# ScalarE and accumulating transfers take over the plain sums of the folded w_down chunks

## The chip, the cores and the metric

The kernel runs on one core of one Trainium2 chip. The metric is the device time of one execution in microseconds (us); lower is better. Of the kernel before there are three timed runs: 1345.83, 1346.43 and 1347.23 us, with a median of 1346.43 us. The profile is of one further execution that took 1346.6 us.

## The reference, cut to what matters

One layer on 256 tokens of width 2048, in float32. A mixing sub-layer with three branches makes a new `x`; then comes a squared-ReLU MLP with hidden width 8192, and a final RMSNorm:

```
h2 = rmsnorm(x, g_mlp)
x = x + jnp.square(jax.nn.relu(h2 @ w_up)) @ w_down
return rmsnorm(x, g_final)
```

The change touches only how parts of the product with `w_down` are added to `x`. The per-token factor of the RMSNorm (its square, since the ReLU is squared) is not applied to `h2` but to the sums of the product with `w_down`; it stands in `stat[:, t, 0:1]`, one value a token, for the token halves `t` = 0 and 1 of 128 tokens each.

## The kernel before, in words

All float32 weights are streamed from HBM once, in pieces of 1 MB (class `W`). A piece is loaded by SyncE (L103) into one of three `raw` buffers. It is then split into a high part, cast by ScalarE to float32r (`hi`, L120), and a rest, subtracted by VectorE (`lo`, L121), in two buffers each. TensorE forms three products (high by high, high by rest, rest by high) and sums them in PSUM.

The MLP is cut into four quarters `q` of the hidden width. A quarter has an up stage (16 pieces of `w_up`, tiles `u`, with `settle` at L190 and L192, then the squared ReLU into `av`, then `yact`) and a down stage (16 pieces of `w_down`). The down stage of the quarters 0 to 2 consists of two chunks `c` of 1024 output columns, each run by `down_folded`; quarter 3 has one such chunk, and its other 1024 columns go through `gemm_tok`.

A folded chunk has eight pieces, `p` = 0 to 7. The even ones are ordinary: 24 matmuls of 512 columns into the tiles `dx` (in the code `xs[0]` and `xs[1]`, one a token half, two PSUM banks each). The odd ones use a 2x2 scheme with seven products instead of eight: 21 matmuls, of which nine go into `dx` and twelve into the four banks of `mb` and `ma`. For these pieces VectorE first makes sums of the raw weights (`t`, L110 to L112), and ScalarE and VectorE split those and the raw ones (`th`, `tl`, `hi`, `lo`, L116 and L117). `t`, `th` and `tl` have one buffer each.

PSUM has four tiles of two banks, and one chunk uses all four. At a chunk's end `down_done` (L734) adds each of the four `dx` banks, times the token's factor, to the residual `xres` on VectorE. ScalarE copies the four banks of `mb` and `ma` out: in quarter 0 straight into `macc` (L684), later into a part sum of 128x512 (L687), which an accumulating transfer from GpSimd's queue adds to `macc` (L688). The part sums lie in the two-buffer groups `cr` and `zs` of the pool `tmp`, which `settle` uses too. `sq` and `mg` are two more groups of that pool; `mg` holds `av` in the up stage. After the last quarter's sums `unfold` combines `macc` into `xres`.

Every engine works its instructions in order. That order is laid down when the kernel is built, by a planner that goes by the program's order and by its own estimates of when things are ready; so the order on VectorE and ScalarE isn't exactly that of the code. `next_w` keeps two pieces prepared ahead, and a load is issued only when a `raw` buffer has been read for the last time.

Of the kernel before, what the change touches and what calls it, by code (L numbers as in the profile page):

```python
# [7 lines left out]
F32 = mybir.dt.float32  # L8
F32R = mybir.dt.float32r
AF = mybir.ActivationFunctionType  # L10
ALU = mybir.AluOpType

P = 128
# [10 lines left out]
NQ = 4  # L24
# [22 lines left out]
def hybrid_trunk(ctx: ExitStack, tc: tile.TileContext, xw_d, gmix_d, xtok_d, wst, wtok, wbr, par_d, wpool_d, bgate_d, gfin_d, out_d):  # L47
    nc = tc.nc
# [6 lines left out]
    tmp = ctx.enter_context(tc.tile_pool(name="tmp", bufs=2))  # L55
# [24 lines left out]
    def four(t):  # L80
        return t.rearrange("p a b -> p (a b)").rearrange("p (k n) -> p k n", n=512)
# [60 lines left out]
    def ps_pair(name):  # L142
        return psum.tile([P, 2, 2 * S], F32, name=name, tag="ps")
# [12 lines left out]
    def next_w():  # L156
        while stream and len(ahead) < 2:
            ahead.append(W(*stream.pop(0)))
        return ahead.pop(0)
# [77 lines left out]
    for n, (k0, k1) in enumerate(zip(cuts, cuts[1:])):  # L237
        if 3 <= n < 6:
            t = wraw.tile([P, KT, P], F32, name=f"xw{n}", tag="raw").rearrange("p a b -> p (a b)")
            t = t[:, 0:2 * STEP].rearrange("p (k n) -> p k n", n=STEP)  # L240
        else:
            t = xcut.tile([P, 2, STEP], F32, name=f"xw{n}", tag="xw")
# [22 lines left out]
    for t, k0, k1 in zip(pieces, cuts, cuts[1:]):  # L265
# [10 lines left out]
        for k in ks:  # L276
            for i in range(NF):
                ps, cols = pfirst[i // 2][:, i % 2, :], slice(i * P, i * P + P)
                if not (last and k == KT - 1):
                    nc.tensor.matmul(ps, fhi[:, k, cols], hact[:, k, :], start=k == 0, stop=False)  # L280
        for k in ks:
            for i in range(NF):
                ps, cols = pfirst[i // 2][:, i % 2, :], slice(i * P, i * P + P)
                nc.tensor.matmul(ps[:, S:2 * S], flo[:, k, cols], hact[:, k, 0:S], start=False, stop=False)
        if last:
            for i in range(NF):
                ps, cols = pfirst[i // 2][:, i % 2, :], slice(i * P, i * P + P)
# [151 lines left out]
    for i in range(8):  # L439
        t = tmp.tile([P, 512], F32, name=f"xt{i}", tag=("sq", "cr", "mg", "zs")[i // 2])  # L440
# [170 lines left out]
    for n, width in enumerate((1024, 512, 512)):  # L611
        banks = fresh_banks(width, f"o{at}")
        gemm_tok(merged, banks, width, ALLK, hooks=hooks[n])
        if n == 0:
            xres, part, stat = (res[name] for name in ("xres", "part", "stat"))
        for c in range(width // 512):
            cols = slice(at, at + 512)
# [23 lines left out]
    def mm3(ps, left, right, start=False, stop=False):  # L641
        nc.tensor.matmul(ps, left[0], right[0], start=start, stop=False)  # L642
        nc.tensor.matmul(ps, left[0], right[1], start=False, stop=False)  # L643
        nc.tensor.matmul(ps, left[1], right[0], start=False, stop=stop)  # L644

    def down_folded(q, c):
        xs = [ps_pair(f"dx{q}_{c}_{t}") for t in range(2)]
        mb, ma = ps_pair(f"mb{q}_{c}"), ps_pair(f"ma{q}_{c}")

        def act(k, t):  # L650
            return yact[:, k, t * P:(t + 1) * P], yact[:, k, S + t * P:S + (t + 1) * P]

        for p in range(8):
            w = next_w()
            hi, lo = four(w.hi), four(w.lo)
            if p in FOLD:
                i = FOLD.index(p)
                a11, a12, a22 = act(2 * p, 0), act(2 * p + 1, 0), act(2 * p + 1, 1)
                s1, s2, s3, s4 = ((sact[:, i, 0, n, :], sact[:, i, 1, n, :]) for n in range(4))
                b11, b21, b22 = ((hi[:, n, :], lo[:, n, :]) for n in range(3))  # L660
                t1, t3, t2, t4 = ((w.thi[:, n, :], w.tlo[:, n, :]) for n in range(4))
                first, last = i == 0, i == len(FOLD) - 1
                own = [(xs[1][:, 0, :], a22, t4), (xs[0][:, 0, :], a12, b21), (xs[0][:, 1, :], s4, b22)]
                shared = [(mb[:, 1, :], s1, t1), (mb[:, 0, :], s3, t3), (ma[:, 1, :], s2, t2), (ma[:, 0, :], a11, b11)]
                if last:
                    for ps, left, right in own:
                        mm3(ps, left, right, False, True)
                for ps, left, right in shared:
                    mm3(ps, left, right, first, last)
                if not last:  # L670
                    for ps, left, right in own:
                        mm3(ps, left, right)
            else:
                for k in range(2):
                    for t in range(2):
                        for h in range(2):
                            mm3(xs[t][:, h, :], act(2 * p + k, t), (hi[:, 2 * k + h, :], lo[:, 2 * k + h, :]),
                                p == 0 and k == 0, p == FOLD[-1] - 1 and k == 1 and t == h == 1)
        down_done(xs, 1024, 1024 * c, (1, 0), False)
        for n, m in enumerate((mb, ma)):  # L680
            for h in range(2):
                d = macc[:, c, 2 * (1 - n) + h, :]
                if q == 0:
                    nc.scalar.copy(d, m[:, h, :])  # L684
                    continue
                part_sum = tmp.tile([P, 512], F32, name=f"ps{q}_{c}_{n}_{h}", tag="zs" if n else "cr")
                nc.scalar.copy(part_sum, m[:, h, :])  # L687
                nc.gpsimd.dma_start(d, part_sum, accum_op=ALU.add)  # L688
# [37 lines left out]
    def scaled(t, cols):  # L726
        square_sum(t, cols, cols.start // 512)
        nc.vector.tensor_mul(fin(t, cols), xres[:, t, cols], gfin[:, cols])

    def down_done(banks, width, at, tokens, last):  # L730
        for c in range(width // 512):
            cols = slice(at + 512 * c, at + 512 * c + 512)
            for t in tokens:
                nc.vector.scalar_tensor_tensor(xres[:, t, cols], banks[t][:, c, :], stat[:, t, 0:1],  # L734
                                               xres[:, t, cols], ALU.mult, ALU.add)
                if last:
                    scaled(t, cols)
# [21 lines left out]
    for q in range(NQ):  # L759
# [17 lines left out]
        for c in range(2 if q < NQ - 1 else 1):  # L777
            down_folded(q, c)
# [107 lines left out]
```

## Time and profile before

| | |
|---|---|
| median of three runs | 1346.43 us |
| profiled execution, its own time | 1346.6 us |
| its span, first to last instruction | 1344.1 us |
| TensorE matmuls, busy | 1334.3 us (99%) |
| VectorE, busy | 1010.1 us (75%) |
| ScalarE, busy | 657.6 us (49%) |
| GpSimd, busy | 21.7 us (2%) |
| granted TensorE clock, mean | 0.999 |

Busy time is that of an engine's own instructions; the issue of a DMA by SyncE or ScalarE isn't counted. A wait is an engine's idle time ahead of an instruction, put down to what ended it. The four quarters' stages lie one behind the other from about 644 us on: in quarter 1, for one, the up stage from 818 to 906 us, chunk 0 from 906 to 948 us and chunk 1 from 948 to 990 us.

### The profile page before, as it was taken

To read this page: it belongs to the slowest core of one execution; us is meant where nothing else is said; L and a number is where in the kernel's file an instruction comes from. 1 tells how busy PE (TensorE), PEld (TensorE's weight loads), DVE (VectorE), ACT (ScalarE), POOL (GpSimd) and SP (SyncE) were. 2 spreads that over 40 slices of the span, in tenths; PEclk is the share of its full clock that TensorE was granted. 3 is DMA by queue.
4 is the path that set the end of the run, shared out by engine and by line. 5 is a ranking of instruction groups with operands and counts; after the bars stand their busy time and mean duration, and the time that the engine had idled before them with its cause. 6 is when DMAs were issued, how large, how long until landed. Compare 5 with 4: busy or idle time off the path is not lost.

```text
span 1344.1 us, 16513 instructions
## 1 busy us (share of the span) xinstructions
PE 1334.3 (99%) x6610; PEld 1128.9 (84%) x6610; DVE 1010.1 (75%) x1273; ACT 657.6 (49%) x800; POOL 21.7 (2%) x47
## 2 busy tenths in 40 slices
PE   9999999999999999999999999999999999999997
PEld 8888888888888888888888888888788888888886
DVE  6779888979766465655667996679866799777967
ACT  7544443434454344344545554455554456544554
POOL 0000000000000000000000000000110001100010
PEclk9999999999999999999999999999999999999999
DMA  9655555656556565565555655555775557755582
GB/s 364 229 188 188 188 188 188 206 192 216 192 185 207 212 205 186 188 235 187 173 188 189 211 195 201 182 199 197 224 225 185 196 209 223 246 189 188 192 273 99
DMA packets 43133, 273.11 MB, mean 203 GB/s; under 512 B 4912, under 2 KB 6064, under 8 KB 12464
## 3 DMA queue, kind: packets, MB, share of 16 engines
q1 hardware_dynamic: 39312, 263.93, 56.5%
q0 software_dynamic: 2880, 5.24, 2.2%
q10 hardware_dynamic: 864, 2.89, 0.6%
q8 instruction: 51, 0.84, 0.2%
q14 instruction: 26, 0.21, 0.0%
HBM read 264.71 MB, written 2.10 MB: 198 GB/s over the span
## 4 chain that ended last, share of the span: by engine, by line
PE 93%; DVE 3%; DMA 2%; issue 1%; ACT 0%; POOLq 0%; POOL 0%; DVEq 0%
PE u L124 17%; PE u L127 9%; PE g L511 6%; PE g L512 6%; PE g L510 6%; PE dx L643 4%; PE dx L642 4%; PE dx L644 4%; PE zc L124 3%; PE o L511 2%; PE o L510 2%; PE o L512 2%; DMA raw<-wtok 2%; PE za L124 2%; PE y L511 2%; PE y L512 2%
## 5 line engine op out<-in xcount | busy, mean ns | idle before, releaser
L120 ACT CAST hi<-raw 128x1024 fp32r<-128x1024 f32 x420 | 423.6, 1050 | 435.9 <-PE g L512 134.4
L121 DVE TENSOR_TENSOR lo<-raw,hi 128x1024 fp32r<-128x1024 f32 x420 | 501.7, 1220 | 176.8 <-ACT hi L120 176.7
L124 PE MATMUL u<-hact,hi 128*128 128x512 f32 x1024 | 245.4, 391 | 0.0
L124 PEld LDWEIGHTS u<-hact,hi 128*128 128x128 f32 x1024 | 187.8, 188 | 36.9 <-ACT ps L687 0.4
L510 PE MATMUL g<-hi,hact 128*128 128x512 f32 x384 | 149.9, 390 | 0.0
L512 PE MATMUL g<-hi,hact 128*128 128x512 f32 x384 | 149.4, 389 | 0.0
L511 PE MATMUL g<-lo,hact 128*128 128x512 f32 x384 | 149.4, 389 | 0.0
L127 PEld LDWEIGHTS u<-hact,lo 128*128 128x128 f32 x1024 | 131.4, 191 | 5.1
L127 PE MATMUL u<-hact,lo 128*128 128x256 f32 x1024 | 133.0, 283 | 0.0
L643 PE MATMUL dx<-lo,yact 128*128 128x512 f32 x252 | 98.8, 392 | 0.2 <-DVE lo L121 0.2
L642 PE MATMUL dx<-hi,yact 128*128 128x512 f32 x252 | 98.9, 392 | 0.0
L644 PE MATMUL dx<-hi,yact 128*128 128x512 f32 x252 | 98.4, 391 | 0.0
L329 DVE SCALAR_TENSOR_TENSOR va<-upad,par,va 128x256 f32<-128x256 f32 x180 | 86.8, 482 | 3.4
L510 PEld LDWEIGHTS g<-hi,hact 128*128 128x128 f32 x384 | 72.1, 188 | 15.0
L511 PEld LDWEIGHTS g<-lo,hact 128*128 128x128 f32 x384 | 72.1, 188 | 14.9
L512 PEld LDWEIGHTS g<-hi,hact 128*128 128x128 f32 x384 | 72.1, 188 | 14.8
L116 ACT CAST th<-t 128x1024 fp32r<-128x1024 f32 x56 | 57.5, 1052 | 33.9 <-issue 16.5
L117 DVE TENSOR_TENSOR tl<-t,th 128x1024 fp32r<-128x1024 f32 x56 | 67.1, 1221 | 8.2 <-ACT th L116 8.2
L192 DVE TENSOR_TENSOR zs_u<-u,cr_u 128x512 f32<-128x512 f32 x32 | 22.1, 691 | 60.6 <-ACT cr_u L190 60.6
L190 ACT COPY cr_u<-u 128x512 f32<-128x512 f32 x32 | 18.8, 588 | 90.6 <-PE u L124 83.4
L642 PEld LDWEIGHTS dx<-hi,yact 128*128 128x128 f32 x252 | 47.3, 188 | 11.5 <-ACT ps L687 0.4
L643 PEld LDWEIGHTS dx<-lo,yact 128*128 128x128 f32 x252 | 47.3, 188 | 10.5 <-DVE lo L121 0.6
(219 smaller groups left out, 1898.1 us busy)
## 6 DMA issues: line engine op xcount, KB each, us to landing
raw<-wtok SPq DMA_DIRECT2D x128, 1024.0 KB, 4.8
raw<-wst SPq DMA_DIRECT2D x93, 1024.0 KB, 4.9
raw<-wbr SPq DMA_DIRECT2D x16, 1024.0 KB, 4.9
xw<-xw SPq DMA_DIRECT2D x7, 768.0 KB, 8.1
macc<-ps POOLq DMA_DIRECT2D x20, 256.0 KB, 7.7
bias<-bgate SPq DMA_DIRECT2D x6, 512.0 KB, 3.6
xt<-xtok SPq DMA_DIRECT2D x8, 256.0 KB, 9.5
xres<-xtok ACTq DMA_DIRECT2D x1, 2048.0 KB, 9.4
```

The source lines that it names most:

```text
L117: fg[0] = nc.vector.tensor_sub(l, r, h.bitcast(F32))
L120: fg[1] = nc.scalar.copy(self.hi[:, ks], self.raw[:, ks])
L121: fg[0] = nc.vector.tensor_sub(self.lo[:, ks], self.raw[:, ks], self.hi[:, ks].bitcast(F32))
L124: nc.tensor.matmul(ps, w.hi[:, k, :], act[:, ak, :], start=start, stop=stop)
L127: nc.tensor.matmul(ps[:, S:2 * S], w.lo[:, k, :], act[:, ak, 0:S], start=False, stop=False)
L329: nc.vector.scalar_tensor_tensor(va[:, i, :], upad[:, i, k:k + S], pcol(C_WDW + i * KA + k), va[:, i, :], ALU.mult, ALU.add)
L510: nc.tensor.matmul(banks[t][:, c, :], left, hi[:, i, cols], start=first, stop=False)
L511: nc.tensor.matmul(banks[t][:, c, :], left, lo[:, i, cols], start=False, stop=False)
L512: nc.tensor.matmul(banks[t][:, c, :], rest, hi[:, i, cols], start=False, stop=last)
L642: nc.tensor.matmul(ps, left[0], right[0], start=start, stop=False)
L643: nc.tensor.matmul(ps, left[0], right[1], start=False, stop=False)
L644: nc.tensor.matmul(ps, left[1], right[0], start=False, stop=stop)
```

## The change

In `down_folded`, for the quarters 0 to 2, the call of `down_done` is replaced. For each of the four `dx` banks ScalarE now writes the bank times the token's factor into a 128x512 buffer `own`, and a transfer from GpSimd's queue adds that buffer to the 512 columns of `xres`. The buffers come from the groups `sq` (token half 1) and `mg` (token half 0), two each. Quarter 3 is as it was.

```diff
--- before.py
+++ after.py
@@ -676,7 +676,15 @@
                         for h in range(2):
                             mm3(xs[t][:, h, :], act(2 * p + k, t), (hi[:, 2 * k + h, :], lo[:, 2 * k + h, :]),
                                 p == 0 and k == 0, p == FOLD[-1] - 1 and k == 1 and t == h == 1)
-        down_done(xs, 1024, 1024 * c, (1, 0), False)
+        if q < NQ - 1:
+            for h in range(2):
+                for t in (1, 0):
+                    own = tmp.tile([P, 512], F32, name=f"ox{q}_{c}_{t}_{h}", tag="sq" if t else "mg")
+                    nc.scalar.activation(own, xs[t][:, h, :], AF.Copy, scale=stat[:, t, 0:1])
+                    cols = slice(1024 * c + 512 * h, 1024 * c + 512 * h + 512)
+                    nc.gpsimd.dma_start(xres[:, t, cols], own, accum_op=ALU.add)
+        else:
+            down_done(xs, 1024, 1024 * c, (1, 0), False)
         for n, m in enumerate((mb, ma)):
             for h in range(2):
                 d = macc[:, c, 2 * (1 - n) + h, :]
```

## Rows read from the trace of the kernel before

**Rows 1.** The page: busy us (share of span) and instructions of an engine.
```profile
PE 1334.3 (99%) x6610; PEld 1128.9 (84%) x6610; DVE 1010.1 (75%) x1273; ACT 657.6 (49%) x800; POOL 21.7 (2%) x47
```
**Rows 2.** Tile dx, all chunks: idle before its instructions (us, times), by releaser.
```profile
  DVE lo L121: 0.9, 2
  ACT ps L687: 0.4, 2
  DVE xres L734: 0.3, 1
  ACT macc L684: 0.2, 1
```
**Rows 3.** Lines L734, L753, L688: duration in ns min/median/max; L688's landing.
```profile
L734 DVE SCALAR_TENSOR_TENSOR xres<-dx,stat,xres x28: 740/744/752, 771.8 to 1292.6; 128x512 f32<-128x512 f32 x28
...
L753 ACT ACTIVATE xres<-xres,stat x2: 722/726/729, 1333.4 to 1338.5; 128x512 f32<-128x512 f32 x2
...
L688 POOL DMA_DIRECT2D macc<-ps x20: 869/1220/1647, 947.6 to 1294.3; - x20
...
DMA to landing us min/median/max: 5.7/7.7/14.8
```
**Rows 4.** ScalarE's order of time, quarter 1, chunk 0 to 1 (start, us, [idle before]).
```profile
942.97 2.00 ACT L120 CAST hi<-raw 128x1024 fp32r<-128x1024 f32 x2 [3.45 <-PE dx L644]
946.45 1.07 ACT L687 COPY ps<-mb 128x512 f32<-128x512 f32 x2 [1.48 <-PE mb L644]
...
950.26 1.51 ACT L116 CAST hi<-raw 128x1536 fp32r<-128x1536 f32 x1
```
**Rows 5.** DMA queues in 952:962: packets, MB, share of 16 engines.
```profile
q0 software_dynamic: 571, 1.04, 57.6%
q1 hardware_dynamic: 261, 1.88, 48.2%
```
**Rows 6.** The chain of waits in 896:975: start, us, what.
```profile
944.72 0.74 DVE xres L734
945.47 2.28 DVE lo L121 x2
947.76 6.28 DMA raw<-wtok
...
957.66 7.56 DMA raw<-wtok
965.32 1.24 DVE t L110
...
967.91 1.23 DVE lo L121
```
**Rows 7.** Issues in 784:785.5, then 1129:1130, then 953:958 (KB each, median us to landing).
```profile
raw<-wtok SPq DMA_DIRECT2D x1, 1024.0 KB, 5.0
...
raw<-wtok SPq DMA_DIRECT2D x1, 1024.0 KB, 6.3
...
raw<-wtok SPq DMA_DIRECT2D x2, 1024.0 KB, 7.9
```
**Rows 8.** The same places of quarters 0 and 2: ScalarE and VectorE in order of time.
```profile
774.40 1.07 ACT L684 COPY macc<-mb 128x512 f32<-128x512 f32 x2 [1.48 <-PE mb L644]
1119.11 1.07 ACT L687 COPY ps<-mb 128x512 f32<-128x512 f32 x2 [1.48 <-PE mb L644]
...
793.28 2.35 DVE L121 TENSOR_TENSOR lo<-raw,hi 128x1024 fp32r<-128x1024 f32 x2
1138.68 2.35 DVE L121 TENSOR_TENSOR lo<-raw,hi 128x1024 fp32r<-128x1024 f32 x2
```
**Rows 9.** The next up stage, quarter 2: GpSimd's issues, their landing, VectorE in order of time.
```profile
989.47 3.59 POOL L688 DMA_DIRECT2D macc<-ps  x4 [38.09 <-ACT ps L687]
...
DMA to landing us min/median/max: 5.7/6.7/8.6
...
1001.80 0.69 DVE L192 TENSOR_TENSOR zs_u<-u,cr_u 128x512 f32<-128x512 f32 x1 [2.78 <-ACT cr_u L190]
```

## The prediction

> **What bounds the kernel now.** I read the page's first part first. TensorE's matmuls are busy 1334.3 us, 99% of the span, beside 75% for VectorE and 49% for ScalarE [rows 1]. So what the change does to the other engines counts only where TensorE then waits, or stops waiting. The second view is the idle time ahead of the instructions on `dx`, the tile whose eviction is changed. Over all seven folded chunks TensorE or its weight loads stood idle for 0.9 + 0.4 + 0.3 + 0.2 = 1.8 us there [rows 2]. Of this 0.3 us is for VectorE's adds to `xres` (L734), which the change removes; 0.6 us is for ScalarE's copies, because a new chunk's `dx` may lie in the banks that these set free; 0.9 us is for `lo`, the prepared weights. Nothing like the VectorE time removed can come back: 1.8 us is the most that better evictions could give here.
>
> The third view is the chain of waits through quarter 1. It does not lead along TensorE there but runs in a loop of weight load, VectorE's sums `t`, VectorE's `lo` and the next load: each load is issued when `lo` has read the buffer that the load will fill (945.47 + 2.28 gives 947.75, and the next load starts at 947.76) [rows 6]. At 967.91 the `lo` of an ordinary piece starts late, because VectorE took the sums of the next folded piece first (965.32) and these had waited for a load of 7.56 us. That is where TensorE's 0.9 us for `lo` arose. So this loop has no slack to spare in chunk 1 of quarter 1, and a slower load there becomes TensorE time.
>
> **The change part by part.**
>
> *VectorE.* It loses 3 quarters x 2 chunks x 4 = 24 adds of 0.744 us [rows 3], 17.9 us of 1010. On the path stands just the first one of a chunk's end: 0.74 us at 944.72, ahead of the `lo` that releases a load [rows 6]. The other three of the four stood behind that `lo`. So the gain on the loop is 0 to 0.74 us at each change from chunk 0 to 1; I take 0.7, as the chain has it.
>
> *ScalarE.* It gains 24 activations of 128x512 out of PSUM with a factor per token. That shape with such a factor isn't in the trace from PSUM. The plain copy out of PSUM takes 1.07 us for two, 0.53 each [rows 4], and the activation with a factor out of SBUF takes 0.726 [rows 3]. I take 0.65, between them; four are 2.1 to 2.9 us, say 2.6. ScalarE is idle for 1.48 us between the casts that end at 944.97 and the first `mb` copy [rows 4], and the last ordinary sums are done by then, as the plain order of the code has them ahead of `mb` and `ma`. That hides 1.5 us; 0.6 to 1.4 us are left, say 1.1. Behind them wait the `mb` and `ma` copies, then `th` and `hi` of the next folded piece, the last of which ends at 951.77 [rows 4] and would end at about 952.9. With it the `lo` after it moves, which releases the load that follows. Net of VectorE's 0.7 the loop shifts by -0.1 to +0.7 us, say +0.4, at each of the three changes from chunk 0 to 1.
>
> *PSUM banks.* The `dx` banks now come free by ScalarE's order, not VectorE's. TensorE's waits for banks were 0.9 us in all [rows 2]; I leave them as they are, with 0 to 0.5 us a chunk for the range in place of their present 0.1 to 0.3.
>
> *GpSimd.* It gains 24 issues of about 1.22 us [rows 3]. Nothing waits for that engine here but its own transfers.
>
> *The transfers.* This is the part with a price. In 952:962 the four accumulating transfers of one chunk end took 57.6% of 16 engines for 10 us, that is 5.8 us of all of them, and with the weight loads' 48.2% the engines were full: the sum is over 100% [rows 5]. The loads beside them took 7.56 us, and 2 x 7.9 - 7.56 = 8.2 us, where one without such company took 5.0 [rows 7]. The change adds as much again at six chunk ends: 24 transfers, 6 x 5.8 = 35 us of all engines. Where does this reach TensorE?
>
> Quarter 1, chunk 1: the loop shifts by 0.4, and the decisive load, 7.56 us now, may take 7.56 to 8.2, as its neighbour did [rows 7]; there is no slack. That is -0.1 to +1.4 us; I take 1.0, nearer the upper end since the company lasts longer.
>
> Quarter 2, chunk 1: the same `lo` starts at 1138.68. The first copy of `mb` tells how far the chunks lie apart: 1119.11 - 946.45 = 172.66 us. So this `lo` was 967.91 + 172.66 - 1138.68 = 1.9 us earlier in its chunk than in quarter 1, where TensorE waited at most 0.9; the slack is about 1.0 us [rows 2, 6, 8]. The load took 6.3 us [rows 7]. A longer stay of 0 to 1.9 (to 8.2) and the shift of 0.4 make 0.4 to 2.3, less 1.0: 0 to 1.3. I take 0.8.
>
> Quarter 0, chunk 1, which has no accumulating transfers now: 946.45 - 774.40 = 172.05 apart, so the `lo` at 793.28 is 2.6 us early, slack 1.7 [rows 6, 8]. Its load would go from 5.0 to between 6.3 and 7.9 [rows 7]: +1.3 to +2.9, with the shift 1.7 to 3.3, less 1.7: 0 to 1.6. I take 0.5.
>
> *The up stage behind chunk 1.* The `macc` transfers now queue behind four others on GpSimd's queue. Their part sums lie in the groups `cr` and `zs`. At the start of quarter 2 the four were issued from 989.47 to 993 and landed 5.7 to 8.6 us after their issue, so by 1000 or so; `zs_u` is written at 1001.80 [rows 9]. With up to 5.8 us in front of them they land by 1006, so this instruction may wait up to 4 us, and behind it on VectorE wait `av` and the `lo` of coming pieces. VectorE was idle for 2.78 us ahead of it [rows 9], so the delay falls in a loose stretch: 0 to 1.5 us of TensorE in quarters 1 and 2 each, and 0 in quarter 0, whose `macc` is copied. I take 0.05 each, nearest to the rows, which show no wait there now.
>
> *Where the trace and a page differ.* The 256 KB transfers of the kernel before took 5.7 to 14.8 us, median 7.7, from issue to landing [rows 3]. The Trainium skill, in "DMA: Bandwidth & Descriptors", section "Anatomy of one DMA — SWDGE (gpsimd) path", fits such a transfer with 2.0 us plus its bytes over 436,000, which an estimate makes 2.6 us for 256 KB, or 2.4 us of data for four. By that page the added transfers would hold the engines 2.4 us an end instead of 5.8, and the sum below would be about +1 instead of +2.4. The measured shares decide.
>
> *The sum.* 1.0 + 0.8 + 0.5 + 0.1 = +2.4 us. The profiled execution took 1346.6 us, so 1349.0; the median of the runs is 0.17 less, so **1348.8 us**. A change of less than 0.2% (2.7 us) can't be told from none on this kernel, so the forecast is: no change that can be told, with a lean to slower. The bounds of the terms above add up to -0.1 on the low side, with all waits for banks (0.9) gone -1.0, and on the high side, with 6 x 0.25 more for banks, to 1.4 + 1.3 + 1.6 + 3.0 + 1.5 = 8.8.
>
> **The rivals.**
>
> *The transfers push the loads back in full.* If the transfer engines work off what GpSimd has queued before they go on with a load, the decisive load moves by the whole 5.8 us of the added four. Then quarter 1 loses 5.8 + 0.4 = 6.2, quarter 2 loses 6.2 - 1.0 = 5.2, quarter 0 loses 6.2 - 1.7 = 4.5: +15.9, 1362 us, slower. It decides from the point where the delay exceeds the slack, 1 to 2 us. For it: in 953:958 a load was 3.2 us late, most of the span of the four transfers [rows 5, 7]. Against it: with 5.8 us of such work the loads lost 2.6 and 3.2 us, not 5.8, and TensorE's waits for `lo` stayed under 1 us. The Trainium skill, in the same page, section "Queues, rings and completion order", has each transfer engine take turns between its queues, a packet at a time, which speaks against it, and no run here shows the turns by themselves. Half of this effect would give +8, about 1354.
>
> *The lighter VectorE loosens the loop.* 17.9 us less on VectorE, and loads issued 0.7 us earlier, could make good what the transfers take, and the waits of [rows 2] go: 0 to -1.8 us, about 1345.5. For it: one of the removed adds is on the chain. Against it: `th` and `hi` of the same stretch are ScalarE's, which gets the work.
>
> *The up stage waits for its buffers.* 1.5 us in two quarters on top of the forecast: +5.4, 1351.8, slower. For it: landing by 1006 against 1001.80. Against it: four PSUM tiles let TensorE run on while `zs_u` is late.
>
> **How the numbers follow.** The forecast, +0.3 to +2.7: 0.42. The loads pushed back, in part or in full: 0.32. The up stage: 0.14. The lighter VectorE: 0.12, of which 0.04 for more than 2.7 us, which the waits in the trace don't hold but an order that the planner changes elsewhere might. So faster 0.04, same 0.42 + 0.08 = 0.50, slower 0.46. The forecast's own range is 1346.7 to 1349.1. The range for 8 in 10 goes from 1345.4 (the sum of the low bounds) to 1356, which takes in the sum of all upper bounds (1355.2) and the push-back up to some 60%; left out are the full push-back and a gain beyond 1.0 us.
>
> **What the profile after would show.** Right: no L734 in quarters 0 to 2, 24 ScalarE activations of 0.59 to 0.73 us, twice the software queue's share behind each chunk, loads of 7 to 9 us there, and TensorE waits for `lo` of 1 to 3 us in sum. Wrong, on the slow side: loads over 10 us and TensorE idle by several us at the third to fifth piece of chunk 1, or VectorE waiting for a DMA at `zs_u`. Wrong, on the fast side: the waits on `dx` gone and a span at or under 1344 us. What would make it wrong altogether is an order on VectorE or ScalarE that the planner changes far from the chunk ends.

## The result and the profile after

The changed kernel takes 1361.64 us (median of four runs, 1360.31 to 1362.80) against 1346.13 us for the kernel before on the same chip. It is slower by 15.5 us, well above the range that was given. The medians' ratio is 1.0115; the recorded estimate is 1.0119, with a 95% interval of 1.0107 to 1.0131. The profiled execution took 1361.13 us, with a span of 1359.4.

The page of the kernel after, busy us of the engines, the queue of GpSimd's transfers (q0; that of the loads is q1), and the median time to landing:

```profile
PE 1339.0 (99%) x6610; PEld 1132.1 (83%) x6610; DVE 993.9 (73%) x1249; ACT 671.2 (49%) x824; POOL 43.2 (3%) x71
...
q0 software_dynamic: 6336, 11.54, 4.7%
...
xres<-ox POOLq DMA_DIRECT2D x24, 256.0 KB, 8.6
...
macc<-ps POOLq DMA_DIRECT2D x20, 256.0 KB, 14.7
```

The change does what it says: VectorE lost 16.2 us, ScalarE gained 13.6, and the software queue moves 11.54 MB. TensorE is still busy for 99% of the span, but the `macc` transfers land 14.7 us after their issue instead of 7.7 [rows 3].

TensorE's 6610 matmuls stand in the same order in both traces, so the start of each can be set against its start before. The distance moves at four places only (worked out from the start times in the two timelines):

```
stretch                           after minus before, us    lost
up to quarter 1, chunk 0          -1.2 (-0.8 of it from the first loads on)
quarter 1, chunk 1, fifth piece   -1.2 ->  2.1              3.3
up stage of quarter 2, 4th piece   2.1 ->  6.2              4.1
quarter 2, chunk 1, fifth piece    6.2 -> 10.8              4.6
up stage of quarter 3, 4th piece  10.7 -> 15.2              4.5
```

That is 16.5 us in four losses of 3.3 to 4.6 us. Quarter 0 loses nothing. What TensorE waited for, in the kernel after (us in total, times, longest):

```profile
PE u L127 <- DVE lo L121: 5.0, 4, 2.3
PE dx L643 <- DVE lo L121: 4.6, 2, 2.7
```

**In chunk 1** it is the loop of [rows 6]. VectorE's order of time there:

```profile
960.66 1.22 DVE L117 TENSOR_TENSOR tl<-t,th 128x1024 fp32r<-128x1024 f32 x1
966.58 1.23 DVE L110 TENSOR_TENSOR t<-raw 128x1024 f32<-128x1024 f32 x1 [4.70 <-DMA raw<-wtok]
967.84 0.69 DVE L111 TENSOR_TENSOR t<-t,raw 128x512 f32<-128x512 f32 x1
968.45 2.35 DVE L121 TENSOR_TENSOR lo<-raw,hi 128x1024 fp32r<-128x1024 f32 x2
```

VectorE waits 4.70 us for the load of the folded piece, and the `lo` that TensorE needs next stands behind that wait. The loads themselves, issued at 956.76 and 1136.61, and the queues' shares in 952:962 (as in [rows 5]):

```profile
raw<-wtok SPq DMA_DIRECT2D x1, 1024.0 KB, 9.7
...
raw<-wtok SPq DMA_DIRECT2D x1, 1024.0 KB, 10.5
...
q0 software_dynamic: 769, 1.41, 79.0%
q1 hardware_dynamic: 165, 1.24, 30.6%
```

The decisive load takes 9.7 us where it took 7.56, and in quarter 2 10.5 where it took 6.3 [rows 7]. GpSimd's transfers hold 79% of the engines' time in a stretch where they held 57.6%. Within it the shares change. In 953:957 a load was issued at 953.4, and the loads had next to nothing (a share is a sum of packet times and can exceed 100%):

```profile
q0 software_dynamic: 447, 0.81, 112.2%
q1 hardware_dynamic: 1, 0.01, 0.5%
```

The kernel before has such a stretch too: in its 954:957 the transfers have 110.7%, and no packet of a load begins, though one was issued at 953.7. The larger difference lies behind it. In 958:966 the loads have 67.8% and the transfers 37.1%, where it was 87.9% and 12.0% before.

**In the up stage** it is the buffers of `settle`. VectorE, ScalarE and TensorE at the start of quarter 2, in order of time:

```profile
998.75 2.36 DVE L121 TENSOR_TENSOR lo<-raw,hi 128x1024 fp32r<-128x1024 f32 x2 [1.93 <-ACT hi L120]
1011.25 0.69 DVE L192 TENSOR_TENSOR zs_u<-u,cr_u 128x512 f32<-128x512 f32 x1 [10.14 <-DMA macc<-ps]
1014.32 3.49 DVE L121 TENSOR_TENSOR lo<-raw,hi 128x1024 fp32r<-128x1024 f32 x3
...
1005.65 0.59 ACT L190 COPY cr_u<-u 128x512 f32<-128x512 f32 x1 [5.99 <-DMA macc<-ps]
...
1013.86 1.29 PE L127 MATMUL u<-hact,lo 128*128 128x256 f32 x8 [1.91 <-DVE lo L121]
```

ScalarE's first copy waits 5.99 us and VectorE's first sum 10.14 us until a part sum's transfer has landed and its buffer is free. The `lo` of coming weights queue behind that sum, and TensorE runs dry. The four transfers here (L696, issued from 992.7 to 997.8), from issue to landing:

```profile
DMA to landing us min/median/max: 12.8/15.1/17.2
```

**After each stall the clock falls.** Windows of the kernel after: length, busy us (instructions) of PE, PEld, DVE, ACT and POOL, TensorE's granted clock, share of the transfer engines, GB/s:

```profile
967.00:969.50 2.50, 0.79 (x4) 0.30 (x2) 2.46 (x3) 1.04 (x1) 0.00 (x0) 1.00 0.53 206
969.50:974.00 4.50, 4.28 (x12) 3.38 (x13) 4.35 (x6) 2.42 (x2) 0.00 (x0) 0.62 0.48 153
...
1013.50:1018.50 5.00, 4.20 (x19) 3.74 (x20) 4.31 (x5) 1.72 (x2) 0.00 (x0) 0.66 0.38 118
...
1150.00:1155.00 5.00, 4.68 (x14) 3.69 (x14) 4.85 (x6) 2.42 (x2) 0.00 (x0) 0.66 0.51 170
...
1194.60:1199.50 4.90, 4.27 (x20) 3.78 (x21) 4.19 (x5) 1.64 (x3) 0.00 (x0) 0.65 0.41 122
```

A mean of 0.62 to 0.66 means that TensorE ran part of the stretch at 1.2 instead of 2.4 GHz. TensorE's order of time shows it: the matmuls of 512 columns are 0.23 us apart before the stall, then 0.42 to 0.43, and 0.23 again:

```profile
967.16 0.39 PE L644 MATMUL dx<-hi,sact 128*128 128x512 f32 x1
967.39 0.40 PE L642 MATMUL dx<-hi,yact 128*128 128x512 f32 x1
969.72 0.50 PE L643 MATMUL dx<-lo,yact 128*128 128x512 f32 x1 [1.94 <-DVE lo L121]
...
971.82 0.63 PE L643 MATMUL dx<-lo,yact 128*128 128x512 f32 x1
972.25 0.63 PE L644 MATMUL dx<-hi,yact 128*128 128x512 f32 x1
...
974.17 0.39 PE L643 MATMUL dx<-lo,yact 128*128 128x512 f32 x1
974.39 0.39 PE L644 MATMUL dx<-hi,yact 128*128 128x512 f32 x1
```

The price is (1 - 0.62) x 4.5 = 1.7 us of work at full clock, and (1 - 0.66) x 5 = 1.7 at the other places: 6.8 us of the 16.5. The stalls themselves cost the other 9.7.

### The profile page after: what moved, and what is told of

It reads as the page before. It is cut to its first block, busy times and chain, and to the rows that moved or that the text cites. A ratio compares the mean times of both kernels' runs of the same rounds, so it can differ in the third digit from the quotient of the medians.

```text
span 1359.4 us, 16583 instructions
## 1 busy us (share of the span) xinstructions
PE 1339.0 (99%) x6610; PEld 1132.1 (83%) x6610; DVE 993.9 (73%) x1249; ACT 671.2 (49%) x824; POOL 43.2 (3%) x71
## 3 DMA queue, kind: packets, MB, share of 16 engines
q0 software_dynamic: 6336, 11.54, 4.7%
## 4 chain that ended last, share of the span: by engine, by line
PE 70%; issue 25%; POOL 2%; DMA 2%; DVE 0%; ACT 0%; SPq 0%; POOLq 0%; DVEq 0%; ACTq 0%
PE u L124 8%; PE g L511 6%; PE g L512 6%; PE g L510 6%; PE u L127 4%; PE zc L124 3%; PE o L511 2%; PE o L510 2%; PE dx L643 2%; PE dx L642 2%; PE o L512 2%; PE dx L644 2%; PE za L124 2%; PE y L511 2%; PE y L512 2%
## 5 line engine op out<-in xcount | busy, mean ns | idle before, releaser
L116 ACT CAST th<-t 128x1024 fp32r<-128x1024 f32 x56 | 57.6, 1057 | 43.2 <-issue 16.4
## 6 DMA issues: line engine op xcount, KB each, us to landing
macc<-ps POOLq DMA_DIRECT2D x20, 256.0 KB, 14.7
```

## The experiments

Each run is set against runs of the kernel before on the same chip, whose medians lay between 1345.39 and 1346.09 us. The theory (T): the added transfers alone cost the time, at two kinds of place: the late loads in chunk 1 of quarters 1 and 2, handed on by VectorE's order, and the part sums that hold the buffers of the next up stage. The rivals: ScalarE's new work (S), late loads at all four places (L), a cost by each transfer (P), and the eighth transfer, which GpSimd holds back (G).

**e1, ScalarE's part without the transfers.**

```diff
-                    nc.gpsimd.dma_start(xres[:, t, cols], own, accum_op=ALU.add)
+                    nc.vector.tensor_add(xres[:, t, cols], xres[:, t, cols], own)
```

> ScalarE scales the ordinary sums out of PSUM as in the change, but VectorE adds them to the residual from SBUF; the 24 added transfers are gone. Theory T (the added transfers: they delay the weight loads in chunk 1 of quarters 1 and 2, and the part sums' landing at the start of the up stages of quarters 2 and 3; TensorE stalls four times by 2 to 3 us and each stall is followed by 3.4 us at half clock): all four stalls go, 1345.5 to 1348.5 us, clock 0.999. Rival S (ScalarE: its 24 more activations make the casts of the next weights late): the stalls stay, 1357 to 1362 us.

Measured: 1344.67 us, ratio 0.9993 (0.9984 to 1.0003). The span and the clock of its trace:

```profile
core 0: 1341.8 us, clock 0.999
```

S falls: the same 24 activations of 0.68 us are there, and not one of the four stalls. TensorE's matmuls wait at the start of the program only, 1.1 us at most.

**e2, the transfers without ScalarE's part.** VectorE adds as before; four transfers more run at each chunk end, into buffers that nobody reads. GpSimd zeroes each buffer first.

```diff
         down_done(xs, 1024, 1024 * c, (1, 0), False)
+        if q < NQ - 1:
+            for h in range(2):
+                for t in (1, 0):
+                    own = tmp.tile([P, 512], F32, name=f"ox{q}_{c}_{t}_{h}", tag="sq" if t else "mg")
+                    nc.gpsimd.memset(own, 0.0)
+                    cols = slice(1024 * c + 512 * h, 1024 * c + 512 * h + 512)
+                    nc.gpsimd.dma_start(own, xres[:, t, cols], accum_op=ALU.add)
```

> The kernel before with its adds on VectorE, plus the same four transfers per chunk end as in the change, with nobody to read what they make: each adds the finished 512 columns of the residual into a buffer that GpSimd has zeroed. ScalarE does nothing more than before. Theory T: the four stalls of the change are there, 1356 to 1363 us, clock 0.994 to 0.997. Rival S: 1345.5 to 1348.5 us. The transfers start some 1 to 2 us later than in the change, as they wait for VectorE, so the stalls may differ by 1 us each.

Measured: 1358.67 us, ratio 1.0100 (1.0083 to 1.0117). Its waits are those of the change:

```profile
PE u L127 <- DVE lo L121: 5.2, 4, 2.4
PE dx L643 <- DVE lo L121: 3.4, 2, 1.8
...
DVE zs_u L192 <- DMA macc<-ps: 20.6, 2, 10.6
```

So the transfers alone make 13.3 us of the 15.5. Matched start by start as above, the parts differ: chunk 1 lost 1.4 and 2.1 us, as the stalls were 1.8 us at most and the clock didn't fall there; the up stages lost 5.0 and 5.6.

**e8, the part sums in other buffers.**

```diff
-                    own = tmp.tile([P, 512], F32, name=f"ox{q}_{c}_{t}_{h}", tag="sq" if t else "mg")
+                    own = tmp.tile([P, 512], F32, name=f"ox{q}_{c}_{t}_{h}", tag="mg" if h == 0 else ("cr" if t else "zs"))
-                part_sum = tmp.tile([P, 512], F32, name=f"ps{q}_{c}_{n}_{h}", tag="zs" if n else "cr")
+                part_sum = tmp.tile([P, 512], F32, name=f"ps{q}_{c}_{n}_{h}", tag="sq" if n == 0 else ("zs" if h else "cr"))
```

> The change with the same order of instructions on every engine; only the buffer groups differ: the sums of dx lie in mg, mg, cr and zs, the part sums of mb and ma in sq, sq, cr and zs, so that the first copy and sum of the up stage find a buffer whose transfer was among the first four, not the last four. Theory T with two places: VectorE's wait of 10 us for a macc transfer at zs_u goes to under 2 us, the stalls in the up stages of quarters 2 and 3 (3.9 and 4.3 us with their half clock) go, those in chunk 1 stay: 1352 to 1355 us. Rival L (late weight loads cause all four stalls, the buffers none): 1360 to 1363 us.

Measured: 1352.16 us, ratio 1.0051 (1.0036 to 1.0066). The sum `zs_u` waits for ScalarE's copy as in the kernel before, no longer for a transfer, and behind the program's start TensorE waits only in the chunks:

```profile
1004.45 0.69 DVE L192 TENSOR_TENSOR zs_u<-u,cr_u 128x512 f32<-128x512 f32 x1 [2.79 <-ACT cr_u L190]
...
PE dx L643 <- DVE lo L121: 5.0, 2, 2.6
```

With the same transfers and the same order on every engine, the up stages lose nothing. L falls.

**e9, `lo` ahead of the sums on VectorE.**

```diff
-            nc.vector.tensor_add(t[:, 0:2, :], ...
-            nc.vector.tensor_add(t[:, 2, :], ...
-            nc.vector.tensor_add(t[:, 3, :], ...
+            with tc.issue_after(fg[0].ins):
+                nc.vector.tensor_add(t[:, 0:2, :], ...
+                nc.vector.tensor_add(t[:, 2, :], ...
+                nc.vector.tensor_add(t[:, 3, :], ...
```

> The change, but VectorE's sums of a folded piece are ordered behind the lo of the ordinary piece before it. In the change VectorE waits 4.7 us for the load of the folded piece at the head of its queue, with the lo that TensorE needs behind it. Theory T1 (it is this order that hands the late load on to TensorE): the stalls in chunk 1 of quarters 1 and 2 go (3.3 and 4.7 us with half clock), those of the up stages stay: 1352 to 1356 us. Rival L1 (the late piece itself is needed at that time): stalls move by one piece and stay, 1358 to 1363 us.

Measured: 1352.34 us, ratio 1.0057 (1.0040 to 1.0074). VectorE's order (the lines have moved by one), and TensorE's only waits after the start:

```profile
964.01 2.36 DVE L122 TENSOR_TENSOR lo<-raw,hi 128x1024 fp32r<-128x1024 f32 x2 [1.47 <-ACT hi L121]
966.73 1.23 DVE L111 TENSOR_TENSOR t<-raw 128x1024 f32<-128x1024 f32 x1 [0.36 <-DMA raw<-wtok]
...
PE u L128 <- DVE lo L122: 4.5, 4, 2.3
```

The load lands as late as before (the sums start at 966.73, in the change at 966.58), but nothing stands behind it: the stalls in chunk 1 are gone. The piece itself is not yet needed then, so L1 falls.

**e10, both remedies** (the edits of e8 and e9 together).

> The change with its 24 transfers, and with both remedies at once: part sums in other buffers, and lo ahead of the sums on VectorE. Theory T with its two places (late loads handed on by VectorE's order, part sums that land late): all four stalls go although the transfers stay, 1344 to 1348 us, clock 0.999. Rival X (the two remedies only shift a delay that the transfers cost anyway, as the engines for transfers are full): what one of them saved comes back, 1350 to 1356 us.

Measured: 1345.27 us, ratio 0.9996 (0.9987 to 1.0004). All transfers are there, the clock is whole, and TensorE's matmuls wait at the start of the program only, 1.1 us at most:

```profile
q0 software_dynamic: 6336, 11.54, 4.8%
...
core 0: 1342.2 us, clock 0.999
```

So 6.3 MB more through the software queue cost nothing once nobody waits for a late landing. X falls.

**e5 and e13, two and three of the four transfers.** The other sums are added by VectorE, as in e1. The edit is that of e5; in e13 the condition is `if h == 0 or t == 1:`.

```diff
+                    if h == 0:
                         nc.gpsimd.dma_start(xres[:, t, cols], own, accum_op=ALU.add)
+                    else:
+                        nc.vector.tensor_add(xres[:, t, cols], xres[:, t, cols], own)
```

> The change with two of the four transfers per chunk end; the other two sums are added by VectorE from ScalarE's buffer. Theory T as a threshold (nothing is lost until a load or a part sum is later than its slack of 1 to 3 us): six transfers in a row make the stalls less than half as long and too short for the half clock, 1346 to 1351 us. Rival P (each transfer costs its share): half of the 16 us, 1352 to 1355 us.

> As e5, with three of the four transfers per chunk end, seven in a row with those for macc. With two of four the decisive load of quarter 1 landed at 965.7 us and nothing was lost, with four at 966.5 at a fall of VectorE's order that began with it, and 16 us were lost. Theory T (thresholds, and the half clock after stalls over 2 us): some of the four stalls are there and short, 1347 to 1354 us. Rival G (it is the eighth transfer, which GpSimd issues only when the first has landed, that costs): as e5, 1344.5 to 1347 us.

Measured: e5 1345.87 us, ratio 1.0002 (0.9993 to 1.0011); e13 1351.47 us, ratio 1.0038 (1.0023 to 1.0053). In e5 VectorE waits 3.07 us for the decisive load and still is in time, with 0.3 us of TensorE lost:

```profile
965.82 1.23 DVE L110 TENSOR_TENSOR t<-raw 128x1024 f32<-128x1024 f32 x1 [3.07 <-DMA raw<-wtok]
...
PE dx L643 <- DVE lo L121: 0.3, 1, 0.3
```

In e13 both places begin to lose:

```profile
PE dx L643 <- DVE lo L121: 3.5, 2, 1.9
...
PE u L127 <- DVE lo L121: 0.8, 2, 0.5
```

Two of four cost 0, three 5, four 15.5 us: a threshold and then a steep rise. P falls; G, which had e13 as fast as e5, falls too.

**e7, more room for descriptors.** In the change GpSimd issues seven transfers in a row and the eighth only when the first has landed:

```profile
992.74 3.72 POOL L696 DMA_DIRECT2D macc<-ps  x3
997.84 0.88 POOL L696 DMA_DIRECT2D macc<-ps  x1 [1.39 <-DMA xres<-ox]
```

```diff
-    nc = bacc.Bacc("TRN2", ..., dynamic_dma_scratch_size=2048)
+    nc = bacc.Bacc("TRN2", ..., dynamic_dma_scratch_size=4096)
```

> The change with twice the room for the transfers' descriptors, so that GpSimd needn't hold the eighth of a chunk end back until the first has landed (it issued it at 953.58, right after a landing at 953.32, and 4.9 us behind the seventh). Theory T: transfer time and order stay, so the four stalls stay within 1 us each: 1359 to 1364 us. Rival G (the held-back transfer is what lands too late): 1350 to 1357 us.

Measured: 1358.15 us, ratio 1.0085 (1.0068 to 1.0101), a little under T's range. All eight are now issued in a row, and TensorE's waits are nearly as they were:

```profile
992.56 4.67 POOL L696 DMA_DIRECT2D macc<-ps  x4
...
PE u L127 <- DVE lo L121: 4.6, 3, 2.3
PE dx L643 <- DVE lo L121: 4.1, 2, 2.1
```

The held-back transfer is at most 3.5 us of the loss, part of it because the clock fell after three stalls here, not four. It isn't the main cause.

**e11 and e12, can more be had?** e11 is the kernel before with the order of e9; e12 is e1 with it.

> The kernel before with the order of e9 alone (lo ahead of the sums), no added transfers. Theory T: before has under 2 us of such waits, so 1343.5 to 1346.5 us, not to be told from before. Rival O (this order itself is worth several us, so e9 gained by something else than the late loads): 1338 to 1342 us.

> e1 (ScalarE scales, VectorE adds from SBUF, no added transfers) with the order of e9. A version that might beat both kernels: what TensorE waits for around the chunk ends is 1 to 2 us, so 1343 to 1345.5 us; beyond that nothing is to be had, as TensorE is busy for 1334 us.

Measured: e11 1345.14 us, ratio 0.9996 (0.9987 to 1.0005); e12 1345.41 us, ratio 0.9996 (0.9987 to 1.0005). Neither can be told from the kernel before. O falls. That e1, e10, e11 and e12 come out at one time speaks for TensorE's own work as the floor (it was busy for 1331.7 us of the 1342.2 in the trace of e10). No version tried beats the kernel before by more than its measurement is uncertain.

## Why the prediction was wrong

The prediction said +2.4 us, no change that can be told. It had the bottleneck, the loop and the direction of the lean right, and mis-sized two terms and left out a third. Both signs on the slow side that it named came: a load over 10 us with TensorE waiting at the fifth piece of chunk 1, and VectorE waiting for a DMA at `zs_u`.

- *VectorE, ScalarE, PSUM banks: right.* The activation takes 0.684 us (forecast 0.65); the decisive load is issued 0.3 us later against TensorE's work (forecast 0.4); TensorE's waits for banks are gone. e1 shows that ScalarE's work and the order of the banks cost nothing, and e10, with VectorE's adds gone too, that nothing comes of these.

- *The transfers beside the loads: the mechanism was right, the size wrong.* The terms were 1.0, 0.8 and 0.5 us for quarters 1, 2 and 0; measured 3.3, 4.6 and 0, of which 1.7 in each of the first two is the clock. The step that failed is the bound on the decisive load, "7.56 to 8.2, as its neighbour did". Both rows came from a stretch with four transfers; they can't bound one with eight, which gave 9.7 and 10.5. A row beside half of the load is a lower end, not an upper one. Quarter 0, with four transfers, kept within its slack, as e5 does with six.

- *The up stage: the largest miss.* The term was 0.05 us in each of two quarters, with 1.5 as a bound; measured 4.1 and 4.5, with the clock. The step that failed is that a late `zs_u` falls in a loose stretch. The wait for `zs_u` was foreseen as up to 4 us and as covered by 2.78 us of idle time. It was 10.1 us, 7.4 more than before, since the last four transfers came behind four others, beside the loads, and landed 12.8 to 17.2 us after their issue, not 5.7 to 8.6 [rows 9]. And the idle time of [rows 9] was no reserve: it lies ahead of that sum, and the `lo` of coming pieces stand behind it. ScalarE's copy ahead of it waited too, 6.0 us, which the prediction did not count. As a rival this place was given 1.5 us in each quarter.

- *The clock: not in the prediction.* In this trace each stall of 1.9 to 2.7 us cost 1.7 us more, because TensorE then worked at half clock for a while. The trace of before could not show it: behind the program's start no wait of its matmuls was over 0.2 us.

- *The rivals.* "The transfers push the loads back in full" ended at 1362 us, which is near the measured time, but not by its parts: it gave quarter 0 4.5 us (measured 0), the chunks of quarters 1 and 2 6.2 and 5.2 (measured 3.3 and 4.6 with the clock), and the up stages nothing (measured 8.6, half of the loss). That the sum came out near is luck. The loads were indeed held off for 3 to 4 us from their issue, but nearly as long before the change; then they went on at two thirds of the engines, and the decisive ones took 2.2 and 4.1 us longer, not 5.8. The lighter VectorE bought nothing: e10, which keeps it and heals the rest, is as fast as before. The prediction's estimate of 2.6 us for such a transfer, from the Trainium skill, "DMA: Bandwidth & Descriptors", section "Anatomy of one DMA — SWDGE (gpsimd) path", doesn't agree with the trace: the added ones, one behind the other and beside loads, took 8.6 us in the median.

## What to carry to other kernels

Where one engine sets the time, an edit that takes work off another engine is worth only what the first waits for; look at who will wait for the new transfer's landing, and for which buffer, before counting what it saves. A delay below the slack is free and one above it is paid in full, so bound it by a stretch with as much company as the change will make, not by one with half. In an in-order queue the instruction to look at is the one behind the wait: moving it ahead, or giving the late transfer a buffer that nobody needs soon, took the whole loss away here with all the transfers still there.

## What was not expected of the hardware

TensorE's granted clock fell to half after stalls of 1.9 to 2.7 us, at each of the four places of the change, and stayed there for a few us of steady work. The length of a stall alone doesn't tell: in e8 the second of two, 2.3 us in the chunk of quarter 2, was followed by no fall (windows of e8, columns as above), while in e13 one of 1.9 us at the same place was (a mean of 0.62 in its 1146:1150.5):

```profile
1145.50:1150.00 4.50, 3.62 (x16) 3.00 (x17) 4.50 (x5) 2.02 (x3) 0.00 (x0) 1.00 0.32 98
1150.00:1155.00 5.00, 5.00 (x24) 4.06 (x23) 4.65 (x5) 2.53 (x3) 0.00 (x0) 1.00 0.62 215
```

Seven accumulating transfers of 128x512 were in flight at once with 2048 bytes for descriptors, and GpSimd stood before the eighth; with 4096 it issued eight in a row. Why the transfer engines leave a load aside for 3 to 4 us and then divide their time between the two kinds of queue was not tested by itself and stays open.
